# A decoder block: seven pairs of up-projection tiles by Strassen's seven products of quarters

## The chip, the cores and the metric

The kernel runs on one core of a Trainium2 chip. A core has five engines that work side by side, each through its own queue in order: TensorE (PE in the profile; its weight loads are shown as PEld), VectorE (DVE), ScalarE (ACT), GpSimd (POOL) and SyncE (SP, which here only issues DMAs). The metric is the device time of one execution in microseconds (us), lower is better.

## The reference

One decoder block on 512 tokens of width 1024, all in float32. The part that matters here is its last third:

```
h2 = rmsnorm(x, norm2_g) * (1 + scale2) + shift2          # (512, 1024)
u  = causal_dwconv(h2 @ w_up, ffn_conv_w, ffn_conv_b)     # (512, 5632), 3 taps along the tokens
u_gate, u_val = u[..., :2816], u[..., 2816:]
x  = x + gate2 * ((silu(u_gate) * u_val) @ w_down)        # (512, 1024)
return rmsnorm(x, final_g)
```

`shift2`, `scale2` and `gate2` are three of six sections of silu(c) @ w_ada + b_ada. Ahead of this part stand the first norm, a recurrent branch, an attention branch, and their merge; neither the diff nor the prediction touches them.

## The kernel before

**Products of two halves.** Every float32 operand of a large product is split into a high and a low part of TensorE's own float32 format. ScalarE copies the value into the high part, which rounds it; VectorE subtracts that from the value and writes the low part (`split`, lines 200 to 205). A product is then three matmuls: high by high, high by low, low by high (`mm3`, lines 233 to 238). For weights this is done on the fly: SyncE loads 128x1024 of raw weights into one of three buffers (`raw`), and each half of 512 columns is split into a buffer of the names `whl` and `whg`, two of each, in turn (`w_both`, `Stream`).

**The up projection.** Its 5632 output channels are 44 tiles of 128 channels by 512 tokens, taken as 22 pairs j = 0 to 21: tile 2j holds gate channels, tile 2j + 1 the value channels that go with them. A tile is 8 pieces of 128 inputs x 3 matmuls = 24 matmuls of 128 weights by 512 tokens, into one bank of PSUM (the tag `acc`, three banks in turn; `fil`, `gm` and `tr` are other banks). The first four tiles go in two halves of 256 tokens, since the second half of h2 is ready later, so their 192 matmuls are 256 columns wide. From tile 4 on, tiles follow each other in the order of the program (`in_order`).

**Behind each tile** comes the convolution: ScalarE scales the tile out of PSUM and adds the bias (L1050), VectorE adds the two other taps, also out of PSUM (L1052, twice). When both tiles of a pair are through, ScalarE makes tanh of half the gate (L1053), VectorE two multiplications (L1054, L1055), and the product is split into `ff`, the stationary operand of the down projection. That is eleven VectorE instructions for a pair: four splits of weights, four taps, two multiplications, one split of the result.

**The second modulation's row.** gate2 (`ada2(1, ...)`, lines 540 to 555) is summed on VectorE from eight loaded blocks of 128x1024, sixteen instructions (L553), then split, summed over the partitions by four matmuls with ones (L562) and copied out (L563). In this kernel the sums are taken up between pairs 2 and 9, the row behind pair 10.

**What sets the order.** Up to the up projection a table of numbers fixes each engine's order (`QUEUES`). From there on a scheduler orders each engine's queue by priority at build time; loads and splits of weights stand some 100 places ahead (`AHEAD`). On the chip each engine then takes its queue strictly in that order.

Of the kernel before, what the change touches and what calls it, by code (L numbers as in the profile page):

```python
# [87 lines left out]
AHE = 100  # L88
SQB = (1, 0, 2, 3)
EARLY = 4  # L90

QUEUES = {
    "PE": """
# [72 lines left out]
def block_kernel(ctx, tc, a):  # L166
# [860 lines left out]
    with phase("p_ffn") as p3:  # L1027
# [4 lines left out]
        for s in (slice(0, T // 2), slice(T // 2, T)):  # L1032
            for m in range(EARLY):
                for k in range(NK):
                    with tc.high_priority(offset=AHE):
                        w, o = wu.get((m * NK + k) * P)
                    with in_order(ORDE):
                        last = mm3(ub[m][:, s], w, o, P, h2[:, k], s, k == 0, k == NK - 1)
                chained = last
        for j in range(NF):  # L1040
            w = st(sb, "Y", 2, [P, 4, T])
            for i in range(2):
                if 2 * j + i < EARLY:
                    b = ub[2 * j + i]
                else:
                    b = bank("acc")
                    project(b, wu, 2 * j + i, NK, lambda k: h2[:, k], ahead=AHEAD, order=ORD)
                cj = i * NF + j
                u = w[:, i, :]
                S.activation(u, b, AF.Identity, scale=vc("fw", 2 * 2 * NF + cj), bias=vc("fb", cj))  # L1050
                for d in (1, 2):
                    V.scalar_tensor_tensor(u[:, d:], b[:, :T - d], vc("fw", (2 - d) * 2 * NF + cj), u[:, d:], MUL, ADD)  # L1052
            S.activation(w[:, 2, :], w[:, 0, :], AF.Tanh, scale=0.5)  # L1053
            V.scalar_tensor_tensor(w[:, 0, :], w[:, 2, :], 1.0, w[:, 0, :], ADD, MUL)  # L1054
            V.scalar_tensor_tensor(w[:, 0, :], w[:, 0, :], 0.5, w[:, 1, :], MUL, MUL)  # L1055
            o = hl(p3, "ff", NF)
            split(o, 0, T, w[:, 0, :])
            ff.append(o)
# [173 lines left out]
```

## Time and profile before

| | us |
|---|---|
| time, median of 3 runs (lowest to highest) | 877.36 (877.22 to 878.44) |
| the profiled execution: its own time | 880.0 |
| the profiled execution: span of its instructions | 878.2 |
| TensorE busy in the span (share) | 858.8 (98%) |
| VectorE busy | 640.6 (73%) |
| ScalarE busy | 488.1 (56%) |

The profile is one execution. "Busy" is the union of an engine's instructions, and instructions of one engine overlap: a matmul of 512 columns has a duration of 0.40 us, yet the next one starts 0.23 us later. So a duration is a latency, and what an instruction takes of its engine is read from the distance between starts. The share of the span says nothing of one stage; views of stretches do. Lines named L... are those of the kernel before, but in rows of the changed program's order they are three to a hundred higher (`split` is L207 and L208 there).

### The profile page before, as it was taken

Reading aid. Unit: us, or ns where it says so; the run is one execution under the profiler, and the core shown is the slowest. Engines: PE = TensorE matmul, PEld = TensorE weight load, DVE = VectorE, ACT = ScalarE, POOL = GpSimd, SP = SyncE. Lnnn points to the kernel's source line nnn. Section 1 sums busy time; section 2 is a strip of 40 time slices with the busy share of each in tenths; the row PEclk is TensorE's granted clock in tenths of the full one; section 3 lists DMA queues with packets and bytes.
Section 4 is the critical chain, followed back from the end, with each engine's and each line's share of the span. In section 5 each row is a group of like instructions: output and inputs, shape, how many; then the busy total and the mean of one; then the engine's idle time right before and its main releaser. Section 6 shows DMA issues by size and latency. Waiting matters only on the chain.

```text
span 878.2 us, 11212 instructions
## 1 busy us (share of the span) xinstructions
PE 858.8 (98%) x4030; PEld 688.6 (78%) x4030; DVE 640.6 (73%) x1212; ACT 488.1 (56%) x896; POOL 18.7 (2%) x43
## 2 busy tenths in 40 slices
PE   7999999999999999999999999999999999999996
PEld 4777888878876777777877898888788888888885
DVE  7979888987966999997456899666666666424434
ACT  7475778667755788884244654444544444322323
POOL 0001000000020000000000000000000000000000
PEclk8999999999999999999999999999999999999999
DMA  9813233344462343454324174333333332333312
GB/s 351 344 67 106 79 103 119 107 137 120 158 174 96 123 138 123 143 191 146 96 72 144 39 277 125 92 93 95 96 97 97 97 96 82 101 92 94 94 66 97
DMA packets 33804, 109.08 MB, mean 124 GB/s; under 512 B 4290, under 2 KB 8002, under 8 KB 33748
## 3 DMA queue, kind: packets, MB, share of 16 engines
q1 hardware_dynamic: 32116, 103.60, 36.0%
q0 software_dynamic: 1632, 4.75, 2.3%
q8 instruction: 32, 0.52, 0.2%
q14 instruction: 24, 0.20, 0.1%
HBM read 103.59 MB, written 2.13 MB: 120 GB/s over the span
## 4 chain that ended last, share of the span: by engine, by line
PE 72%; DVE 10%; ACT 8%; DMA 7%; issue 3%; POOL 0%; SPq 0%; DVEq 0%; ACTq 0%; POOLq 0%
PE acc L237 9%; PE acc L238 9%; PE acc L236 9%; PE tr L238 3%; PE tr L236 3%; PE tr L237 3%; PE acc L834 2%; PE acc L836 2%; PE acc L835 2%; DMA wa<-in_w_adat 2%; PE tr L738 2%; PE tr L1098 2%; PE tr L1100 2%; PE tr L1099 2%; PE gm L236 2%
## 5 line engine op out<-in xcount | busy, mean ns | idle before, releaser
L205 DVE TENSOR_TENSOR whg<-raw,whg 128x512 fp32r<-128x512 f32 x119 | 81.6, 688 | 86.8 <-ACT whg L204 86.5
L204 ACT ACTIVATE whl<-raw 128x512 fp32r<-128x512 f32 (+2 forms) x131 | 75.2, 576 | 110.8 <-PE acc L238 29.5
L204 ACT ACTIVATE whg<-raw 128x512 fp32r<-128x512 f32 x119 | 74.2, 627 | 98.5 <-PE acc L238 58.6
L205 DVE TENSOR_TENSOR whl<-raw,whl 128x512 fp32r<-128x512 f32 (+2 forms) x131 | 81.3, 621 | 56.2 <-ACT whl L204 55.9
L236 PE MATMUL acc<-A,whg 128*128 128x512 f32 x176 | 70.0, 398 | 0.0
L237 PE MATMUL acc<-A,whg 128*128 128x512 f32 x176 | 69.5, 395 | 0.0
L238 PE MATMUL acc<-A,whg 128*128 128x512 f32 x176 | 69.5, 395 | 0.0
L1052 DVE SCALAR_TENSOR_TENSOR Y<-acc,vec,Y 128x511 f32<-128x511 f32 x86 | 64.4, 749 | 1.3
L238 PE MATMUL acc<-A,whl 128*128 128x512 f32 x160 | 63.2, 395 | 0.0
L237 PE MATMUL acc<-A,whl 128*128 128x512 f32 x160 | 63.2, 395 | 0.0
L236 PE MATMUL acc<-A,whl 128*128 128x512 f32 x160 | 63.1, 395 | 0.0
L715 ACT ACTIVATE P<-P,mx,qsc 128x512 f32<-128x512 f32 (+3 forms) x64 | 41.2, 645 | 17.5 <-DVE mx L711 17.5
L236 PEld LDWEIGHTS acc<-A,whg 128*128 128x128 f32 x176 | 33.0, 187 | 8.4 <-issue 0.2
L238 PEld LDWEIGHTS acc<-A,whg 128*128 128x128 f32 x176 | 33.0, 187 | 8.1
L237 PEld LDWEIGHTS acc<-A,whg 128*128 128x128 f32 x176 | 33.0, 188 | 8.0 <-issue 0.2
L1050 ACT ACTIVATE Y<-acc,vec 128x512 f32<-128x512 f32 x43 | 32.8, 763 | 6.5 <-PE acc L238 6.5
L237 PEld LDWEIGHTS acc<-A,whl 128*128 128x128 f32 x160 | 30.1, 188 | 7.3
L238 PEld LDWEIGHTS acc<-A,whl 128*128 128x128 f32 x160 | 30.0, 188 | 7.1
L236 PEld LDWEIGHTS acc<-A,whl 128*128 128x128 f32 x160 | 30.0, 188 | 7.1
L236 PE MATMUL gm<-A,whg 128*128 128x512 f32 x88 | 35.5, 404 | 0.0
L237 PE MATMUL gm<-A,whg 128*128 128x512 f32 x88 | 35.3, 401 | 0.0
L238 PE MATMUL gm<-A,whg 128*128 128x512 f32 x88 | 35.2, 400 | 0.0
(509 smaller groups left out, 2276.0 us busy)
## 6 DMA issues: line engine op xcount, KB each, us to landing
raw<-in_w_up SPq DMA_DIRECT2D x44, 512.0 KB, 3.5
raw<-in_w_dn SPq DMA_DIRECT2D x22, 512.0 KB, 3.5
wa<-in_w_adat SPq DMA_DIRECT2D x16, 512.0 KB, 9.4
raw<-in_w_adat SPq DMA_DIRECT2D x16, 512.0 KB, 3.3
raw<-in_w_xr SPq DMA_DIRECT2D x10, 512.0 KB, 3.8
raw<-in_w_pr SPq DMA_DIRECT2D x10, 512.0 KB, 3.6
raw<-in_w_gm SPq DMA_DIRECT2D x8, 512.0 KB, 3.6
raw<-in_w_gr SPq DMA_DIRECT2D x8, 512.0 KB, 3.5
```

The costliest lines, as they stand in the source:

```text
L204: S.activation(h, src, AF.Copy)
L205: return V.tensor_tensor(dst[:, 1, lo_c:lo_c + n], src, h.bitcast(F32), SUB).ins
L236: PE.matmul(out, wh, x[:, 0, xs], start=start, stop=False)
L237: PE.matmul(out, wh, x[:, 1, xs], start=False, stop=False)
L238: return PE.matmul(out, wl, x[:, 0, xs], start=False, stop=stop).ins
L715: S.activation(pq, pq, AF.Exp, scale=qsc[:, qb:qb + 1], bias=mx[:, qb:qb + 1], accum_out=sm[:, qb:qb + 1])
L738: PE.matmul(yb[:, kb * P:], vv, pth[:, part, off:off + n], start=(i == 0 and part == 0), stop=(i == 3 and part == 1))
L834: PE.matmul(out, lt[:, 0, s], w[:, 0, :], start=start, stop=False)
L835: PE.matmul(out, lt[:, 0, s], w[:, 1, :], start=False, stop=False)
L836: return PE.matmul(out, lt[:, 1, s], w[:, 0, :], start=False, stop=stop).ins
L1050: S.activation(u, b, AF.Identity, scale=vc("fw", 2 * 2 * NF + cj), bias=vc("fb", cj))
L1052: V.scalar_tensor_tensor(u[:, d:], b[:, :T - d], vc("fw", (2 - d) * 2 * NF + cj), u[:, d:], MUL, ADD)
```

## The change

In pairs j = 5, 7, 9, 11, 13, 15 and 17 the two tiles together, 256 channels by 1024 inputs by 512 tokens, are computed by Strassen's method (Winograd's form of it): weights and h2 are each taken as 2x2 quarters, and seven products of quarters stand in for eight. A product of quarters is 4 pieces x 3 matmuls = 12 matmuls of 256 columns. Four of the seven need sums of quarters of h2 (T1 to T4), computed once during pairs 0 to 3; four need sums of quarters of the weights, computed for each pair. Six products run as one group (`front`); the seventh runs after the gate tile of the next, ordinary pair (`last_product`), because it adds onto a bank that VectorE has to read first. The pair's tiles are put together in SBUF, so the taps of such a pair read SBUF instead of PSUM. The sums for gate2 move from pairs 2 to 9 to pairs 18 to 21, two blocks for each pair, and its row from behind pair 10 to behind pair 21.

```diff
+STRASSEN = (5,7,9,11,13,15,17)
+G2J = 18
+ROOM = -1
...
+        def h_whole(e, n):
+            o = st(p3, "ff", NF, [P, HK, HT])
+            V.tensor_tensor(o, h2[:, HK * e:HK * e + HK, 0, tok2[n]].bitcast(F32),
+                            h2[:, HK * e:HK * e + HK, 1, tok2[n]].bitcast(F32), ADD)
+            return o
...
+        def t_parts():
+            b12, t1 = h_whole(0, 1), h_whole(0, 0)
+            V.tensor_tensor(t1, b12, t1, SUB)
+            yield t_part(t1, p3, "ff", NF)
+            t3 = h_whole(1, 1)
+            V.tensor_tensor(t1, t3, t1, SUB)
+            yield t_part(t1, p3, "ff", NF)
+            V.tensor_tensor(t3, t3, b12, SUB)
+            yield t_part(t3, sb, "R", 4)
+            t4 = h_whole(1, 0)
+            V.tensor_tensor(t4, t4, t1, SUB)
+            yield t_part(t4, sb, "R", 4)
...
+        def prod(out, w, x, start, stop):
+            for k, (xk, s) in enumerate(x):
+                wh, wl = w[:, 0, k * P:k * P + P], w[:, 1, k * P:k * P + P]
+                for e, (we, xe) in enumerate(((wh, 0), (wh, 1), (wl, 0))):
+                    last = PE.matmul(out, we, xk[:, xe, s], start=start and k == 0 and e == 0,
+                                     stop=stop and k == HK - 1 and e == 2, skip_group_check=True).ins
+            return last
+
+        def weights(j):
+            with tc.high_priority(offset=AHEAD):
+                r0, r1 = raw(), raw()
+                dma(r0, a["w_up"][2 * j])
+                dma(r1, a["w_up"][2 * j + 1])
+                w11, w12, w21, w22 = r0[:, :T], r0[:, T:], r1[:, :T], r1[:, T:]
+                s1 = st(p3, "ff", NF, [P, T])
+                q11, q12 = quarter(j, w11), quarter(j, w12)
+                V.tensor_tensor(s1, w21, w22, ADD)
+                V.tensor_tensor(w21, w11, w21, SUB)
+                V.tensor_tensor(w11, s1, w11, SUB)
+                qs1, qs2 = quarter(j, s1), quarter(j, w11)
+                V.tensor_tensor(w12, w12, w11, SUB)
+                qs4, qs3, q22 = quarter(j, w12), quarter(j, w21), quarter(j, w22)
+            return q11, q12, qs1, qs2, qs4, qs3, q22
+
+        def front(w, q11, q12, qs1, qs2, qs4, qs3, q22):
...
+            with in_order():
+                prod(x, q11, h_part(0, 0), True, False)
+                prod(y_, q12, h_part(1, 0), True, True)
+                S.activation(p1, x, AF.Copy)
+                prod(z, qs1, Ts[0], True, False)
+                V.tensor_tensor(w[:, 0, :HT], y_, p1, ADD)
+                prod(x, qs2, Ts[1], False, False)
+                S.activation(p5, z, AF.Copy)
+                prod(z, qs4, h_part(1, 1), False, True)
+                S.activation(p2, x, AF.Copy)
+                V.tensor_tensor(w[:, 0, HT:], z, p2, ADD)
+                chained = prod(x, qs3, Ts[2], False, False)
+                V.tensor_tensor(w[:, 1, HT:], x, p5, ADD)
+            return x, q22
+
+        def last_product(w, x, q22):
+            nonlocal chained
+            with in_order():
+                chained = prod(x, q22, Ts[3], False, True)
+            S.activation(w[:, 1, :HT], x, AF.Copy)
...
         for j in range(NF):
             w = st(sb, "Y", 2, [P, 4, T])
+            if j in STRASSEN:
+                left = (j, w) + front(w, *ahead)
+                continue
+            convs = []
             for i in range(2):
...
+                if left and i == 0:
+                    last_product(*left[1:])
+                    for e in range(2):
+                        conv(left[0], e, left[1][:, 2 + e, :], left[1][:, e, :])
+                    gate(left[1][:, 2, :], left[1][:, 3, :], left[1][:, 0, :])
+                    left = None
+                if i and j + 1 in STRASSEN:
+                    ahead = weights(j + 1)
+                convs.append((j, i, w[:, i, :], b))
+            for c in convs:
+                conv(*c)
+            gate(w[:, 0, :], w[:, 1, :], w[:, 2, :])
+            if j < 4:
+                Ts.append(next(t_it))
-            if j == 2:
+            if j == G2J:
                 g2_it = ada2(1, st(sb, "acc4", 1, [P, D]), lambda: st(sb, "R", 4, [P, D]))
-            if 2 <= j < 10:
+            if G2J <= j < G2J + 4:
+                next(g2_it)
                 g2 = next(g2_it)
-            if j == 10:
+            if j == G2J + 3:
                 ada_row(g2, 1.0)
```

`quarter` splits one quarter of weights into the next `whl` or `whg`; `t_part` splits a T into two tiles; `conv` and `gate` are the instructions of before, put into functions.

The order on TensorE around pair 11 of the changed kernel follows. acc_5857, tr_5858 and tr_5859 are the banks of the Strassen pair, acc_5939 and acc_5997 the gate and value tile of pair 12; ff_4897 to ff_4920 and R_5005 to R_5094 are T1 to T4.

```order
L1099 MATMUL acc_5857<-A_4366,whl_5819 128x256 x12
L1099 MATMUL tr_5858<-A_4366,whg_5822 128x256 x12
L1099 MATMUL tr_5859<-ff_4897,whl_5828 128x256 x6
L1099 MATMUL tr_5859<-ff_4898,whl_5828 128x256 x6
L1099 MATMUL acc_5857<-ff_4919,whg_5831 128x256 x6
L1099 MATMUL acc_5857<-ff_4920,whg_5831 128x256 x6
L1099 MATMUL tr_5859<-A_4366,whl_5835 128x256 x12
L1099 MATMUL acc_5857<-R_5005,whg_5838 128x256 x6
L1099 MATMUL acc_5857<-R_5006,whg_5838 128x256 x6
...
L1099 MATMUL acc_5857<-R_5093,whl_5841 128x256 x6
L1099 MATMUL acc_5857<-R_5094,whl_5841 128x256 x6
L239 MATMUL acc_5997<-A_4366,whl_6000 128x512
```

Where 48 matmuls of 512 columns stood there are 72 of 256, then (where the line of dots is) the gate tile of pair 12, then the last 12 and the value tile.

VectorE's queue of the kernel before around one pair of the same stretch; Y_5984 is the pair that is being finished, Y_5905 the one before it, whl_6067 to whg_6106 are weights of the next.

```order
L1055 SCALAR_TENSOR_TENSOR Y_5905<-Y_5905 128x512
L205 TENSOR_TENSOR whl_6067<-raw_6065,whl_6067 128x512
L205 TENSOR_TENSOR ff_5981<-Y_5905,ff_5981 128x512
L205 TENSOR_TENSOR whg_6070<-raw_6065,whg_6070 128x512
L1052 SCALAR_TENSOR_TENSOR Y_5984<-acc_5985,vec_84,Y_5984 128x511
L1052 SCALAR_TENSOR_TENSOR Y_5984<-acc_5985,vec_84,Y_5984 128x510
L205 TENSOR_TENSOR whl_6103<-raw_6101,whl_6103 128x512
L1054 SCALAR_TENSOR_TENSOR Y_5984<-Y_5984 128x512
L205 TENSOR_TENSOR whg_6106<-raw_6101,whg_6106 128x512
L1052 SCALAR_TENSOR_TENSOR Y_5984<-acc_6021,vec_84,Y_5984 128x511
L1052 SCALAR_TENSOR_TENSOR Y_5984<-acc_6021,vec_84,Y_5984 128x510
```

Splits of weights stand singly between the taps and the multiplications here, with one to three other instructions between one and the next.

The same queue in the changed kernel, from the split of pair 13's second quarter to that of its fourth. Y_5856 is Strassen pair 11, Y_5938 the ordinary pair 12 (its value tile is acc_5997), raw_6030 and raw_6031 are pair 13's raw weights. Its first row is the split of whl_6038, the second quarter; whg_6044 is the third, whl_6047 the fourth.

```order
L208 TENSOR_TENSOR whl_6038<-raw_6030,whl_6038 128x512
L1151 SCALAR_TENSOR_TENSOR Y_5938<-acc_5939,vec_84,Y_5938 128x510
...
L1155 SCALAR_TENSOR_TENSOR Y_5938<-Y_5938 128x512
L1151 SCALAR_TENSOR_TENSOR Y_5856<-Y_5856,vec_84 128x510
L1156 SCALAR_TENSOR_TENSOR Y_5856<-Y_5856 128x512
L1112 TENSOR_TENSOR ff_6034<-raw_6031 128x512
L208 TENSOR_TENSOR ff_5994<-Y_5856,ff_5994 128x512
...
L208 TENSOR_TENSOR whg_6044<-ff_6034,whg_6044 128x512
L1114 TENSOR_TENSOR raw_6030<-ff_6034,raw_6030 128x512
L1151 SCALAR_TENSOR_TENSOR Y_5938<-acc_5997,vec_84,Y_5938 128x511
L1116 TENSOR_TENSOR raw_6030<-raw_6030 128x512
L208 TENSOR_TENSOR whl_6047<-raw_6030,whl_6047 128x512
```

The dots stand for one tap of Y_5856 and for the sum of L1113. Between the second and the fourth quarter of a pair VectorE now finishes two pairs of tiles and forms four sums of weights; before, a split of weights had at most three other instructions ahead of it since the last one.

## Rows read from the trace of the kernel before

**Rows 1.** The page: engine totals, and TensorE, VectorE, clock in 40 slices.

```profile
PE 858.8 (98%) x4030; PEld 688.6 (78%) x4030; DVE 640.6 (73%) x1212; ACT 488.1 (56%) x896; POOL 18.7 (2%) x43
...
PE   7999999999999999999999999999999999999996
...
DVE  7979888987966999997456899666666666424434
...
PEclk8999999999999999999999999999999999999999
```

**Rows 2.** Two stretches: busy us (instructions) of each engine, clock, DMA share, GB/s.

```profile
523.00:545.00 22.00, 22.00 (x97) 17.74 (x96) 22.00 (x36) 11.15 (x18) 0.00 (x0) 1.00 0.44 136
545.00:761.00 216.00, 216.00 (x929) 173.67 (x928) 145.07 (x210) 96.95 (x155) 0.00 (x0) 1.00 0.31 93
```

**Rows 3.** TensorE in order of time: first matmuls of two pairs, 48 apart.

```profile
630.31 0.39 PE L236 MATMUL acc<-A,whl 128*128 128x512 f32 x1
...
641.49 0.39 PE L236 MATMUL acc<-A,whl 128*128 128x512 f32 x1
```

**Rows 4.** TensorE in order of time: 256 columns, 50 matmuls apart.

```profile
500.00 0.28 PE L237 MATMUL acc<-A,ff 128*128 128x256 f32 x1
...
505.88 0.28 PE L236 MATMUL acc<-A,ff 128*128 128x256 f32 x1
```

**Rows 5.** VectorE in order of time where it never waits.

```profile
522.22 0.75 DVE L1052 SCALAR_TENSOR_TENSOR Y<-acc,vec,Y 128x511 f32<-128x511 f32 x1
522.88 0.69 DVE L1055 SCALAR_TENSOR_TENSOR Y<-Y 128x512 f32<-128x512 f32 x1
523.48 0.69 DVE L205 TENSOR_TENSOR whl<-raw,whl 128x512 fp32r<-128x512 f32 x1
...
528.52 0.75 DVE L553 SCALAR_TENSOR_TENSOR acc<-R,cact,acc 128x512 f32<-128x512 f32 x1
529.18 0.69 DVE L1055 SCALAR_TENSOR_TENSOR Y<-Y 128x512 f32<-128x512 f32 x1
```

**Rows 6.** One tile's turn: last matmul of a buffer, ScalarE's split, VectorE's.

```profile
630.07 0.40 PE L238 MATMUL acc<-A,whg 128*128 128x512 f32 x1
...
630.50 0.63 ACT L204 ACTIVATE whg<-raw 128x512 fp32r<-128x512 f32 x1 [1.33 <-PE acc L238]
631.04 0.76 ACT L1050 ACTIVATE Y<-acc,vec 128x512 f32<-128x512 f32 x1
...
631.17 0.69 DVE L205 TENSOR_TENSOR whg<-raw,whg 128x512 fp32r<-128x512 f32 x1 [1.27 <-ACT whg L204]
```

**Rows 7.** VectorE: two taps of one tile, the second waiting for the first.

```profile
631.84 1.53 DVE L1052 SCALAR_TENSOR_TENSOR Y<-acc,vec,Y 128x511 f32<-128x511 f32 x2
```

**Rows 8.** Groups by shape: other widths on VectorE and ScalarE, and the sums for gate2.

```profile
L322 DVE TENSOR_TENSOR crow<-ident,cact 128x1024 f32<-128x1024 f32 x1 | 1.2, 1225 | 0.1
...
L1120 DVE TENSOR_TENSOR Y<-acc,acc 128x256 f32<-128x256 f32 x1 | 0.4, 425 | 0.4 <-PE acc L1100 0.4
...
L204 ACT ACTIVATE pt<-tr 128x256 fp32r<-128x256 f32 x16 | 6.1, 381 | 1.4 <-PE tr L725 1.2
...
L553 DVE SCALAR_TENSOR_TENSOR acc<-R,cact,acc 128x512 f32<-128x512 f32 x16 | 11.6, 746 | 1.5 <-DMA R<-in_w_ada 1.5
```

**Rows 9.** ScalarE at the first convolution, in order of time.

```profile
514.74 0.78 ACT L1050 ACTIVATE Y<-acc,vec 128x512 f32<-128x512 f32 x1 [4.45 <-PE acc L238]
...
519.15 1.28 ACT L1053 ACT_TABLE_LOAD   x1 [0.81 <-DVE Y L1052]
```

**Rows 10.** TensorE in order of time: the first matmul of pairs 2 and 5.

```profile
523.00 0.40 PE L236 MATMUL acc<-A,whl 128*128 128x512 f32 x1
...
556.57 0.39 PE L236 MATMUL acc<-A,whl 128*128 128x512 f32 x1
```

**Rows 11.** The page: DMA issues, KB each, median us to landing.

```profile
raw<-in_w_up SPq DMA_DIRECT2D x44, 512.0 KB, 3.5
```

More of the change, by code (lines that the diff above doesn't have):

```diff
@@ L1039, in block_kernel, with h_part, t_part @@
                 chained = last
+        HT, HK = T // 2, NK // 2
+        tok2 = (slice(0, HT), slice(HT, T))
+        def h_part(e, n):
+            return [(h2[:, HK * e + k], tok2[n]) for k in range(HK)]
+        def h_whole(e, n):
[3 more added lines that the diff above has]
+            return o
+        def t_part(src, pool, tag, bufs):
+            o = [hl(pool, tag, bufs) for _ in range(2)]
+            for i in range(2):
+                split(o[i], 0, T, src.rearrange("p k n -> p (k n)")[:, i * T:i * T + T])
+            return [(o[k // 2], slice(k % 2 * HT, k % 2 * HT + HT)) for k in range(HK)]
@@ new lines, in block_kernel @@
+        Ts = []
+        def t_parts():
[10 more added lines that the diff above has]
+            yield t_part(t4, sb, "R", 4)
@@ new lines, in block_kernel, with quarter @@
+        t_it = t_parts()
+        nq = [0]
+        def quarter(j, src):
+            nq[0] += 1
+            w = hl(p3, "ff", NF) if j <= ROOM else w_both(nq[0])
+            split(w, 0, T, src)
+            return w
+        def prod(out, w, x, start, stop):
[5 more added lines that the diff above has]
+            return last
@@ new lines, in front @@
+        def front(w, q11, q12, qs1, qs2, qs4, qs3, q22):
+            nonlocal chained
+            X, Y_, Z = bank("acc"), bank("tr"), bank("tr")
+            x, y_, z = (b[:, :HT] for b in (X, Y_, Z))
+            p1, p2, p5 = w[:, 2, :HT], w[:, 2, HT:], w[:, 3, :HT]
+            with in_order():
[12 more added lines that the diff above has]
+            return x, q22
@@ new lines, in last_product, with conv @@
+        def last_product(w, x, q22):
+            nonlocal chained
+            with in_order():
+                chained = prod(x, q22, Ts[3], False, True)
+            S.activation(w[:, 1, :HT], x, AF.Copy)
+        def conv(j, i, u, src):
+            cj = i * NF + j
+            S.activation(u, src, AF.Identity, scale=vc("fw", 2 * 2 * NF + cj), bias=vc("fb", cj))
+            for d in (1, 2):
+                V.scalar_tensor_tensor(u[:, d:], src[:, :T - d], vc("fw", (2 - d) * 2 * NF + cj), u[:, d:], MUL, ADD)
@@ L1040, in block_kernel, with gate @@
+        def gate(u0, u1, t):
+            S.activation(t, u0, AF.Tanh, scale=0.5)
+            V.scalar_tensor_tensor(u0, t, 1.0, u0, ADD, MUL)
+            V.scalar_tensor_tensor(u0, u0, 0.5, u1, MUL, MUL)
+            o = hl(p3, "ff", NF)
+            split(o, 0, T, u0)
+            ff.append(o)
+        left = None
         for j in range(NF):
             w = st(sb, "Y", 2, [P, 4, T])
+            if j in STRASSEN:
+                left = (j, w) + front(w, *ahead)
+                continue
+            convs = []
@@ L1047, in block_kernel @@
                     project(b, wu, 2 * j + i, NK, lambda k: h2[:, k], ahead=AHEAD, order=ORD)
[L1048 to L1058, printed above, removed]
-            if j == 2:
+                if left and i == 0:
[3 more added lines that the diff above has]
+                    gate(left[1][:, 2, :], left[1][:, 3, :], left[1][:, 0, :])
+                    left = None
+                if i and j + 1 in STRASSEN:
[7 more added lines that the diff above has]
+            if j == G2J:
                 g2_it = ada2(1, st(sb, "acc4", 1, [P, D]), lambda: st(sb, "R", 4, [P, D]))
-            if 2 <= j < 10:
+            if G2J <= j < G2J + 4:
+                next(g2_it)
                 g2 = next(g2_it)
-            if j == 10:
+            if j == G2J + 3:
                 ada_row(g2, 1.0)
```

## Prediction

> **What bounds the kernel now.** I read the page first: TensorE is busy 98% of the span, VectorE 73%, and the clock stands at its full level in nearly all slices [rows 1]. An average over stages says little, so next I took the busy time by stretches. From 523 to 761 us, where most of the pairs run, TensorE has no idle time at all (22.00 of 22 us, then 216.00 of 216) at a granted clock of 1.00; VectorE is busy 145.07 of 216 us, ScalarE 96.95 [rows 2]. So in this stage only two things move the time: the slots that matmuls take of TensorE, and any new wait of TensorE for the other engines. VectorE has 33% in reserve there, and spends part of it on waits.
>
> **TensorE's slots.** The first matmuls of two pairs, 48 matmuls of 512 columns apart, stand at 630.31 and 641.49: 11.18 us for a pair, 0.233 each [rows 3]. A Strassen pair has 7 products of 4 x 3 matmuls, 84 of 256 columns. Such matmuls are in the trace: fifty of them take 505.88 - 500.00 = 5.88 us, 0.1176 each [rows 4], so 84 take 9.88. That is 1.30 us less for each pair, 9.1 for seven. If 256 columns took exactly half of 512 it would be 84 x 0.1165 = 9.78, and 9.8 for seven.
>
> **What VectorE gets.** Instructions of VectorE overlap: in a stretch without waits they last 0.69 to 0.75 us, but start 0.60 apart, or 0.66 where the operation takes a column of `vec` as its scalar (522.22 to 522.88, then 523.48; the same 0.66 with all operands in SBUF, 528.52 to 529.18) [rows 5]. An ordinary pair has eleven: 4 x 0.66 + 7 x 0.60 = 6.8, some 7.3 with the dependent ones. A Strassen pair and the ordinary pair after it have 13 splits, 4 sums of weights and 4 multiplications (21 x 0.60), 8 taps (x 0.66), and three sums of 256 columns (0.34 each, estimated below): 18.9 us, in 9.88 + 11.18 = 21.06 us of TensorE. Before it was 2 x 7.3 in 22.36. It still fits, at 90%, so what decides is whether single splits come in time.
>
> **The tight place of each pair.** Let a Strassen pair start at 0. Its products take 12 x 0.1176 = 1.41 each; six end at 8.47, the next gate tile at 14.06, the seventh product at 15.47, the value tile and with it the period at 21.07. The order shows that the second quarter of the next Strassen pair goes into the buffer that the seventh product reads. That buffer's turn is in the trace: the last matmul from it starts at 630.07 and ends at 630.47, ScalarE's split starts at 630.50, VectorE's at 631.17, so 0.70 after the end [rows 6]. Thus VectorE's split of the second quarter starts at 15.64 + 0.70 = 16.34. Behind it in VectorE's queue the order of the changed kernel has, itself included, thirteen instructions before the split of the fourth: 9 x 0.60 + 4 x 0.66 = 8.04. Among them are two multiplications and a split that wait for a result of the instruction just before or for ScalarE. Two dependent taps last 1.53 together with 0.75 for the second one, so the first takes 0.78 instead of 0.66 [rows 7]; I add 0.45 for three such places. With 0.73 for the split itself the low part of the fourth quarter is ready at 16.34 + 8.04 + 0.45 + 0.73 = 25.56. It is needed by the third matmul of the fourth product: 21.07 + 3 x 1.41 + 2 x 0.1176 = 25.55. The margin is nil, and a wait in the dependent places can only be larger than I have put it. The fifth quarter comes out at 26.65 for 26.97. I take 0.2 us late for each of the six pairs 7 to 17: **+1.2**, between 0 and 7.2 (1.2 late each, worked out at the third rival).
>
> **The early pairs.** T1 to T4 put eight VectorE instructions of 128x1024 and eight splits into pairs 0 to 3. One such instruction alone lasts 1.225 [rows 8], of which 0.085 overlap the next (0.69 - 0.60), so 1.14; 256 columns last 0.425, so 0.34. That is 9.1 + 4.8 = 13.9 us, where the sums for gate2, 16 x 0.66 = 10.6 us over pairs 2 to 9, leave. The convolutions begin at 514.74, and ScalarE loads its table for tanh at 519.15 for 1.28 us [rows 9]. Two places are close. The bank that tile 7 takes needs the second tap of pair 2's gate tile; pair 2 starts at 523.00 and pair 5 at 556.57 [rows 10], so tile 7 starts at 523.00 + 3 x 5.59 = 539.8, and VectorE's queue up to that tap, at the same prices, ends at 539.9: **+0.15** (0 to 1). And from the first tap (right behind the first bias, 514.74 + 0.78 and 0.03 for the hand-off, 515.55) to the split of pair 5's fifth quarter VectorE has 65 instructions, 8 x 1.14 + 18 x 0.66 + 39 x 0.60 = 44.4 us, plus 3.3 of waits (2.1 for table and tanh, 1.2 for dependent ones and buffers). That ends at 563.25, and with up to 0.2 for the result of the last one I take 563.4. Pair 5 begins 0.15 late, at 556.72 + 0.03, and its fifth product needs the low part 5.65 + 0.24 later, at 562.64: **+0.8** (0 to 3: nothing where the waits are a quarter shorter; 3 where the wide ones cost their whole 1.225, which adds 0.7, and the waits are 5 us).
>
> **The end.** The sums for gate2 now stand in pairs 18 to 21: 7.3 + 4 x 0.66 = 9.9 us of VectorE for each 11.18. The blocks for them, as the raw weights, are asked for far ahead; raw weights land 3.5 us after their issue [rows 11], and a Strassen pair takes the same two. What is left is that the row's matmuls stand in TensorE's queue behind sums that end late: ScalarE's split is ready within 0.1 us of when it is needed. **+0.3** (0 to 1.3).
>
> **Sum.** -9.1 + 0.15 + 0.8 + 1.2 + 0.3 = -6.65. The profiled execution took 880.0 (span 878.2), 0.3% above the median of 877.36; it would become 873.35, and the median 870.7.
>
> **The rivals.**
>
> *Everything is hidden.* The dependent waits are smaller than I put them, and VectorE catches up where it had idle time: -9.1, or 868.3. For it: 10% of VectorE stays free. Against it: a margin of nil at the fourth quarter. Chance 0.17.
>
> *ScalarE's order costs more.* ScalarE copies partial sums out of PSUM between the products. A copy of 256 columns lasts 0.38 [rows 8], but stands in the queue behind splits that take 0.54 (630.50 to 631.04, [rows 6]). VectorE's sum then stands behind the copy and the next splits behind the sum. The splits of the fifth and sixth product are ready only 0.25 and 0.28 early by my walk, so one more split ahead of a copy makes them late. Half a microsecond for each of seven pairs is 3.5: -6.65 + 3.5 = -3.2, or 874.2. Against it: ScalarE is busy less than half of the stage [rows 2]. Chance 0.15.
>
> *VectorE becomes the bound, and the kernel slower.* Place: the same chain of thirteen before the fourth quarter. If these instructions, many of which now follow one on which they depend, cost their whole duration (0.69 and 0.75, [rows 5]) and not the distance, the chain is 13 x 0.09 = 1.2 us longer, so six pairs lose 7.2; pair 5 loses 65 x 0.09 = 5.9. -9.1 + 0.15 + 5.9 + 7.2 + 0.3 = +4.4, or 881.8. It decides from the point where the fourth quarter is late by more than 1 us in each pair. For it: the dependent taps at 0.78 [rows 7]. Against it: neighbours without dependence do start 0.60 apart [rows 5], and the new splits and sums are mostly such. Chance 0.10.
>
> The Trainium skill ("VectorE: DVE Perf Modes", section on the DRAIN) states a rule for this rival: the next operation does not start until the pipe is empty, though one that is not held starts earlier. By its first half every instruction would cost its duration and the time would be this rival's; for neighbours without dependence this trace shows its second half, 0.60 of 0.69.
>
> That the pair still takes the old number of columns is excluded by the order, which has 84 half-width matmuls for 96. The remaining 0.06 goes to mixtures beyond these.
>
> **How the numbers follow.** My forecast has 0.52, and its own range by its bounds is about 868.5 to 873.5. With the first two rivals in it the range is 867.6 (everything hidden and 256 columns at exactly half: -9.8) to 876.0; the slower rival and part of the rest, under 0.2, lie outside. A difference of 0.2%, 1.75 us, is about what measurement can tell from none. Faster by more: the forecast, the first rival, most of the second, 0.80. Slower: most of the third and a little of the rest, 0.10. Between: 0.10.
>
> **What would show it.** In the new trace pairs 7 to 17 should have 84 matmuls 0.118 apart and a period of 21.1 to 21.5 us from one Strassen pair to the next, against 22.36. TensorE's idle time should stand before the third matmul of the fourth product, ended by VectorE's split, and be 0 to 0.5 us for each pair; in pair 5 some 0.8, before the fifth. If idle time is ended by ScalarE, or its place is the fifth or sixth product in all pairs, the second rival is at work. If VectorE is never idle and its starts are 0.69 and more apart, it is the third. The forecast is wrong if the 256-column matmuls take over 0.125 each (0.6 us more a pair) or the median lies above 876.

## The result and the profile after

The changed kernel takes 873.79 us (median of 9 runs) against 878.44 us for the kernel before, run beside it: a ratio of 0.9948 (95% interval 0.9935 to 0.9961), so 4.6 us faster. One of the nine runs, 1176.41 us at a granted clock of 0.655, is left out of the ratio. The forecast was 870.7, with a range of 867.6 to 876.0.

Below is the page of the changed kernel: engine totals, VectorE's busy tenths in 40 slices, and the shares of the chain that ended last.

```profile
PE 852.0 (97%) x4282; PEld 695.0 (79%) x4282; DVE 682.4 (78%) x1298; ACT 513.5 (59%) x953; POOL 18.7 (2%) x43
...
DVE  6988888998965999997465779999999899424434
...
PE 52%; DVE 25%; ACT 9%; DMA 7%; issue 5%; POOL 0%; SPq 0%; ACTq 0%; DVEq 0%; POOLq 0%
```

VectorE's slices 26 to 34 now read 9 and once 8, where 6 stood [rows 1], and a quarter of the chain runs over VectorE (10% before). The stretches of [rows 2], after:

```profile
523.00:545.00 22.00, 21.85 (x99) 17.55 (x98) 21.53 (x31) 12.46 (x21) 0.00 (x0) 1.00 0.29 93
...
545.00:761.00 216.00, 214.44 (x1201) 184.58 (x1200) 192.78 (x310) 121.61 (x211) 0.00 (x0) 1.00 0.35 118
```

The clock is 1.00 as before; VectorE is busy 89% instead of 67%. TensorE's idle time (1.56 us here) understates its waits, since a waiting matmul lets the one ahead of it run out. So I counted the distance between matmuls on both sides of each place and took off the slots between. One ordinary stretch shows how it reads. These are TensorE's rows of pair 11, each product's twelve matmuls in one row:

```profile
623.79 1.58 PE L1099 MATMUL acc<-A,whl 128*128 128x256 f32 x12
625.21 1.56 PE L1099 MATMUL tr<-A,whg 128*128 128x256 f32 x12
626.61 1.58 PE L1099 MATMUL tr<-ff,whl 128*128 128x256 f32 x12
628.02 1.88 PE L1099 MATMUL acc<-ff,whg 128*128 128x256 f32 x12
629.73 1.58 PE L1099 MATMUL tr<-A,whl 128*128 128x256 f32 x12
631.16 1.59 PE L1099 MATMUL acc<-R,whg 128*128 128x256 f32 x12
632.59 0.40 PE L239 MATMUL acc<-A,whl 128*128 128x512 f32 x1
```

Five products take 1.40 to 1.43 us to the next start; the fourth takes 1.71, so it waited about 0.3 us inside. VectorE's queue of the same stretch says for what (the dots leave out taps, multiplications, sums and splits that follow each other with gaps of 0.1 us at most):

```profile
619.20 0.68 DVE L208 TENSOR_TENSOR whg<-raw,whg 128x512 fp32r<-128x512 f32 x1
...
626.45 0.74 DVE L1151 SCALAR_TENSOR_TENSOR Y<-acc,vec,Y 128x511 f32<-128x511 f32 x1
627.11 0.68 DVE L1116 TENSOR_TENSOR raw<-raw 128x512 f32<-128x512 f32 x1
627.71 1.28 DVE L208 TENSOR_TENSOR whg<-raw,whg 128x512 fp32r<-128x512 f32 x2
```

The first of the last two `whg` splits is the fourth quarter's. From the second quarter's split (619.20) to it are 8.51 us; the walk of the prediction had 8.04 + 0.45 = 8.49. The first pair and the second lose more. Pair 5, in its fifth product:

```profile
563.92 0.50 PE L1099 MATMUL tr<-A,whg 128*128 128x256 f32 x2
564.95 1.45 PE L1099 MATMUL tr<-A,whg 128*128 128x256 f32 x10 [0.53 <-DVE whg L208]
```

Two matmuls run, the third waits for VectorE's low part: 1.03 us from 563.92 instead of 0.24. Another 0.3 us was lost in the fourth product. Pair 7, TensorE, and below it ScalarE:

```profile
583.10 1.63 PE L1099 MATMUL tr<-ff,whl 128*128 128x256 f32 x12
585.36 1.81 PE L1099 MATMUL acc<-ff,whg 128*128 128x256 f32 x12 [0.63 <-ACT Y L1129]
```

```profile
583.88 1.15 ACT L207 ACTIVATE whg<-raw 128x512 fp32r<-128x512 f32 x2 [1.58 <-DVE raw L1114]
584.94 0.37 ACT L1129 ACTIVATE Y<-acc 128x256 f32<-128x256 f32 x1
```

The fourth product adds onto the bank of the first, which ScalarE must have copied out (L1129). The copy stands behind two splits of weights, and these wait for a sum on VectorE (L1114).

The table sums the places. Each number is a distance less its slots; for Strassen pairs also less 0.1 us, which the pairs without a wait in the third experiment show.

| us | forecast | measured |
|---|---|---|
| slots of TensorE, seven pairs | -9.1 | -8.5 |
| bank of tile 7 | +0.15 | +0.3 |
| pair 5 | +0.8 | +1.2 |
| pair 7 | +0.2 | +1.1 |
| pairs 9 to 17, 0.13 to 0.30 each | +1.0 | +1.1 |
| the row of gate2 | +0.3 | +0.5 |
| sum | -6.65 | -4.3 |

The sum agrees with the 4.6 us of the runs. The row's 0.5 us hangs on a transfer that came late in this profiled run (experiment 4). The two profiled executions differ by 3.4 only (span 878.2 to 874.8), because the one of after reached pair 2 a microsecond later (523.98 against 523.00 in [rows 10]) through a part that the change does not touch.

### The profile page after: what moved, and what is told of

Read it like the earlier page. It is cut to its first block, busy times and chain, and to the rows that moved or that the text cites. A ratio compares the mean times of both kernels' runs of the same rounds, so it can differ in the third digit from the quotient of the medians.

```text
span 874.8 us, 11864 instructions
## 1 busy us (share of the span) xinstructions
PE 852.0 (97%) x4282; PEld 695.0 (79%) x4282; DVE 682.4 (78%) x1298; ACT 513.5 (59%) x953; POOL 18.7 (2%) x43
## 4 chain that ended last, share of the span: by engine, by line
PE 52%; DVE 25%; ACT 9%; DMA 7%; issue 5%; POOL 0%; SPq 0%; ACTq 0%; DVEq 0%; POOLq 0%
DVE whg L208 4%; DVE whl L208 3%; DVE Y L1151 3%; PE tr L241 3%; PE tr L240 3%; PE tr L239 3%; PE acc L241 2%; PE acc L239 2%; PE acc L240 2%; DMA raw<-in_w_up 2%; PE acc L837 2%; PE acc L839 2%; PE acc L838 2%; PE tr L741 2%; PE tr L1228 2%
## 5 line engine op out<-in xcount | busy, mean ns | idle before, releaser
L208 DVE TENSOR_TENSOR whl<-raw,whl 128x512 fp32r<-128x512 f32 (+2 forms) x138 | 85.6, 624 | 49.7 <-ACT whl L207 49.3
L208 DVE TENSOR_TENSOR whg<-raw,whg 128x512 fp32r<-128x512 f32 x126 | 85.7, 687 | 37.3 <-ACT whg L207 37.0
L239 PE MATMUL acc<-A,whg 128*128 128x512 f32 x120 | 47.9, 399 | 0.0
L240 PE MATMUL acc<-A,whg 128*128 128x512 f32 x120 | 47.4, 395 | 0.0
L241 PE MATMUL acc<-A,whg 128*128 128x512 f32 x120 | 47.4, 395 | 0.0
L1151 DVE SCALAR_TENSOR_TENSOR Y<-acc,vec,Y 128x511 f32<-128x511 f32 (+1 forms) x58 | 42.9, 744 | 3.6 <-ACT Y L1149 3.5
L239 PE MATMUL acc<-A,whl 128*128 128x512 f32 x104 | 41.1, 396 | 0.1
L240 PE MATMUL acc<-A,whl 128*128 128x512 f32 x104 | 41.1, 395 | 0.0
L241 PE MATMUL acc<-A,whl 128*128 128x512 f32 x104 | 41.1, 395 | 0.0
L239 PE MATMUL tr<-A,whl 128*128 128x512 f32 x80 | 32.6, 408 | 1.4 <-ACT whl L207 1.4
L241 PE MATMUL tr<-A,whl 128*128 128x512 f32 x80 | 32.2, 402 | 1.6 <-DVE whl L208 1.4
L711 DVE CUSTOM_DVE_ANT_0 P<-acc,mask 128x384 f32<-128x384 f32 (+3 forms) x64 | 28.6, 485 | 4.5 <-PE acc L708 4.1
L240 PE MATMUL tr<-A,whl 128*128 128x512 f32 x80 | 31.6, 394 | 0.0
L208 DVE TENSOR_TENSOR pt<-tr,pt 128x512 fp32r<-128x512 f32 (+1 forms) x48 | 27.4, 596 | 2.2 <-ACT pt L207 1.6
L741 PE MATMUL tr<-pt,v 128*128 128x512 f32 (+3 forms) x128 | 28.2, 328 | 0.1
L207 ACT ACTIVATE ff<-Y 128x512 fp32r<-128x512 f32 x22 | 13.9, 631 | 23.8 <-DVE Y L1156 23.1
```

The lines of the kernel that those rows point to most:

```text
L207: S.activation(h, src, AF.Copy)
L208: return V.tensor_tensor(dst[:, 1, lo_c:lo_c + n], src, h.bitcast(F32), SUB).ins
L239: PE.matmul(out, wh, x[:, 0, xs], start=start, stop=False)
L240: PE.matmul(out, wh, x[:, 1, xs], start=False, stop=False)
L241: return PE.matmul(out, wl, x[:, 0, xs], start=False, stop=stop).ins
L711: V.tensor_tensor_reduce(out=pt[:, POFF[qd]:POFF[qd] + n], in0=sc[qd], in1=mask[:, T - n:], scale=1.0, scalar=-3e38, op0=ADD, op1=ALU.max, ...
```

## The experiments

Theory 1: TensorE's slots give all they promise, and what comes back is VectorE being late at these places. The rivals: ScalarE's order, VectorE's load as such, or the moved sums. Ratios are to the kernel before, with 95% intervals; "waits" are distances as above, from one profiled run each. "Changed kernel" is the one of the prediction.

**1. The moved sums alone.**

```diff
-STRASSEN = (5,7,9,11,13,15,17)
+STRASSEN = ()
-            if j < 4:
+            if j < 4 and STRASSEN:
```

> Only the sums for gate2 are moved to pairs 18 to 21; no Strassen pair, no T1 to T4. Theory 1 (the saving of 9.1 us in TensorE's slots is made in full, and 4 to 4.5 us of it come back at five places in the second half of the program: the bank of tile 7, 0.3; pair 5, 1.0; pair 7, 1.1; a wait of 0.17 to 0.32 in each of pairs 9 to 17, 1.3; the row of gate2 behind pair 21, 0.6): here only the last place is left, so TensorE waits 0.5 to 0.7 us at the row and nowhere else from pair 2 on, and the time is 0.4 to 0.8 us above the kernel before. Theory 2 (the move itself costs much, since the sums collide with the last pairs): 2 us or more above. Theory 3 (the row is hidden, the wait belongs to the Strassen pairs): no wait at the row, 0 +- 0.4.

Ratio 1.0009 (0.9998 to 1.0019). No wait at the row or anywhere else from pair 2 on. But the edit did not put the sums where its text says. These are the sixteen sums for gate2 in the kernel before, in this run and in the changed kernel (shortest, median and longest in ns, then the first and the last start):

```profile
L553 DVE SCALAR_TENSOR_TENSOR acc<-R,cact,acc x16: 742/745/752, 512.1 to 542.5; 128x512 f32<-128x512 f32 x16
```

```profile
L556 DVE SCALAR_TENSOR_TENSOR acc<-R,cact,acc x16: 742/745/752, 510.9 to 542.0; 128x512 f32<-128x512 f32 x16
```

```profile
L556 DVE SCALAR_TENSOR_TENSOR acc<-R,cact,acc x16: 740/743/751, 703.6 to 736.1; 128x512 f32<-128x512 f32 x16
```

The kernel before has them around pairs 0 to 3, not from pair 2 to 9, and without Strassen pairs they stand there still, whatever pair the program names: the scheduler orders the queue. Only in the changed kernel are they in pairs 18 to 21. So this run moved the row alone, and of the three theories on the sums it decides none.

**2. The same with T1 to T4.**

```diff
-STRASSEN = (5,7,9,11,13,15,17)
+STRASSEN = ()
```

> As the run before, but with the sums T1 to T4 of quarters of h2 and their splits in pairs 0 to 3, which nothing reads: no Strassen pair. Theory 1: the T parts cost TensorE 0.3 us at tile 7's bank, where VectorE's second tap of pair 2's gate tile comes late, and almost nothing else since pair 5 is an ordinary pair again; with the row 0.8 to 1.2 us above the kernel before. Theory 2 (VectorE is so full in pairs 0 to 4 that the T parts alone delay several tiles): more than one wait between pairs 2 and 5 and 2 to 3 us above.

Ratio 1.0005 (0.9996 to 1.0013). The sums for gate2 start at 565.3 to 595.9 us here, so this run too says nothing of their place at the end. One wait, 0.30 us at tile 7's bank (541.06 in the changed kernel, 539.77 here). So that term belongs to the T sums alone, as the walk had it, and they delay nothing else while no Strassen pair follows.

**3. Two VectorE instructions fewer in each pair**, since the second tap of the Strassen pairs' tiles is left out; this kernel does not compute the block.

```diff
-                        conv(left[0], e, left[1][:, 2 + e, :], left[1][:, e, :])
+                        conv(left[0], e, left[1][:, 2 + e, :], left[1][:, e, :], (1,))
```

(`conv` takes the taps as an argument.)

> The changed kernel without the second tap in the fourteen tiles of Strassen pairs: two VectorE instructions fewer in each pair, and one or two fewer between the split of the second and that of the fourth quarter. The convolution of these tiles lacks one tap. Theory 1 (VectorE's queue of thirteen instructions behind a buffer that comes free late sets the wait of the fourth product): the waits of 0.17 to 0.32 us in pairs 9 to 17 disappear, pair 7's falls below 0.6, and the time is 1.5 to 2.3 us below the changed kernel, some 6.3 us below the kernel before. Theory 2 (ScalarE's order of copies and splits sets it): the waits stay within 0.1 us, and the time is within 0.5 us of the changed kernel. Theory 3 (VectorE's total load is the bound): TensorE gains the whole 1.3 us of each pair's two taps, up to 9 us.

Ratio 0.9928 (0.9915 to 0.9940). Tile 7 (0.3) and pair 5 (1.2) are as they were; all waits of pairs 7 to 17 and of the row are gone. TensorE in pair 11:

```profile
623.72 1.58 PE L1099 MATMUL tr<-ff,whl 128*128 128x256 f32 x12
625.14 1.60 PE L1099 MATMUL acc<-ff,whg 128*128 128x256 f32 x12
626.57 1.58 PE L1099 MATMUL tr<-A,whl 128*128 128x256 f32 x12
```

and the splits of the third and fourth quarter on VectorE:

```profile
621.43 0.69 DVE L208 TENSOR_TENSOR whl<-ff,whl 128x512 fp32r<-128x512 f32 x1
...
623.89 0.68 DVE L208 TENSOR_TENSOR whg<-raw,whg 128x512 fp32r<-128x512 f32 x1
```

The fourth product takes 1.43 again. The split starts 2.98 us behind the pair's first matmul (620.91), where it was 3.92; with 0.73 for itself it has to start by 3.75. ScalarE has as many copies and splits as before, so its load was not the cause, in pair 7 neither (its order is the same but for a few instructions that the scheduler moved by some places). The pairs that wait for nothing also give the clean saving. The first matmuls of the gate tiles of pairs 8 and 18:

```profile
587.15 0.40 PE L239 MATMUL acc<-A,whl 128*128 128x512 f32 x1
...
692.89 0.40 PE L239 MATMUL acc<-A,whl 128*128 128x512 f32 x1
```

These are 5 periods of 21.15 us, 1.21 less than 2 x 11.18 [rows 3]; seven are 8.5.

**4. The row of gate2 later.**

```diff
             if j == G2J + 3:
-                ada_row(g2, 1.0)
...
+            if k == 5:
+                ada_row(g2, 1.0)
```

> The changed kernel with the row of gate2 (split, four matmuls with ones, copy) put behind the fifth piece of the down projection instead of ahead of it. Theory 1: the wait of 0.5 to 0.6 us at the first of these matmuls goes, and no other comes, since gate2 is read only behind the first half of the down projection: 0.5 to 0.6 us below the changed kernel. Theory 3 (the wait is only moved to what follows, because VectorE is late there anyway): another wait of 0.4 us or more near the end of the up projection or the start of the down projection, and no change of the time.

Ratio 0.9943 (0.9929 to 0.9956): by time alone no difference from the changed kernel can be told. In the trace the wait at the row is gone and none has come instead. But the edit need not be the reason. In the changed kernel VectorE stood idle ahead of the first sum, until its block of weights had landed; here, with the same order of VectorE's queue up to that sum, it did not. First the changed kernel (issue and sum), then this run:

```profile
697.15 6.26 SPq L552 DMA_DIRECT2D R<-in_w_ada  x3
703.56 0.75 DVE L556 SCALAR_TENSOR_TENSOR acc<-R,cact,acc 128x512 f32<-128x512 f32 x1 [1.48 <-DMA R<-in_w_ada]
```

```profile
694.55 6.26 SPq L552 DMA_DIRECT2D R<-in_w_ada  x3
699.28 0.75 DVE L556 SCALAR_TENSOR_TENSOR acc<-R,cact,acc 128x512 f32<-128x512 f32 x1
```

The first sum starts 6.41 us after the issue there and 4.73 here. From it to the last block's first sum VectorE has 50 instructions in both: 31.18 us without a gap there, 32.42 us here. So it makes up some 1.2 of the delay, and the rest is the wait of 0.5 at the row. Experiments 5 and 9 have the row in its old place and no idle time ahead of the first sum, and wait less than 0.1 us at it. So the 0.5 us come from one late transfer. The traces of experiments 3, 6, 7 and 8 have such idle time ahead of the first sum too (1.5 to 3.2 us), and of these 7 waits at the row, 3 and 6 do not (8 has the row later); what makes the transfer late in some runs stays open.

**5. The T sums on GpSimd**, which is idle there.

```diff
-            V.tensor_tensor(t1, b12, t1, SUB)
+            G.tensor_tensor(t1, b12, t1, SUB)
```

(and so for all eight.)

> The eight sums of 128x1024 for T1 to T4 are computed by GpSimd instead of VectorE. Theory 1 (VectorE's 9 us for them in pairs 0 to 5 make tile 7's bank 0.3 us late and pair 5's fifth quarter 1.2 us late, and the backlog is still there in pair 7): the wait at tile 7 goes, pair 5's falls from 1.2 to below 0.4, pair 7's from 1.1 to that of pair 9 (0.2 to 0.3), and the steady waits of pairs 9 to 17 stay: 1.5 to 2.3 us below the changed kernel, if GpSimd takes under 5 us for each sum (they are needed some 45 us after h2). Theory 2 (pairs 5 and 7 are late because of their own order of copies and splits on ScalarE, not of the T sums): those two waits stay within 0.2 us, gain 0.3 us. Against both: GpSimd's sums slow VectorE's instructions beside them (then VectorE's 0.60 between starts grows there), or come so late that ScalarE's splits of T block its queue: slower than the changed kernel.

Ratio 0.9973 (0.9963 to 0.9984), 2.2 us slower than the changed kernel. The mishap named last came true. GpSimd, then VectorE beside it:

```profile
528.79 2.41 POOL L1076 TENSOR_TENSOR ff<-ff,ff 128x1024 f32<-128x1024 f32 x1 [8.98 <-DVE ff L208]
531.28 2.74 POOL L1078 TENSOR_TENSOR ff<-ff,ff 128x1024 f32<-128x1024 f32 x1
533.99 2.85 POOL L1058 TENSOR_TENSOR ff<-A 128x1024 f32<-128x1024 f32 x1
```

```profile
528.57 0.74 DVE L1151 SCALAR_TENSOR_TENSOR Y<-fil,vec,Y 128x510 f32<-128x510 f32 x1
529.35 2.40 DVE L1156 SCALAR_TENSOR_TENSOR Y<-Y 128x512 f32<-128x512 f32 x1
531.67 2.90 DVE L208 TENSOR_TENSOR whg<-raw,whg 128x512 fp32r<-128x512 f32 x1
534.49 0.74 DVE L1151 SCALAR_TENSOR_TENSOR Y<-acc,vec,Y 128x511 f32<-128x511 f32 x1
535.15 2.23 DVE L208 TENSOR_TENSOR ff<-Y,ff 128x512 fp32r<-128x512 f32 x1
```

VectorE's instructions with two tensors in SBUF last about as long as GpSimd's beside them, 2.2 to 2.9 us instead of 0.69; those that read a tensor from PSUM keep their 0.74. Tile 7 then waits 0.75 and pair 5 3.7 us; pair 7's wait falls to 0.15.

**6. The sums of weights on GpSimd.**

```diff
-                V.tensor_tensor(s1, w21, w22, ADD)
+                G.tensor_tensor(s1, w21, w22, ADD)
```

(and so for all four.)

> The four sums of quarters of weights of each Strassen pair are computed by GpSimd instead of VectorE; T1 to T4 stay on VectorE. Theory 1 (the chain of thirteen VectorE instructions before the fourth quarter sets the steady wait): three of them leave, 1.8 us, so the waits of pairs 9 to 17 go as in the run with one tap left out, 1.1 us in all, and pair 7's 1.1 falls below 0.5; the row's 0.5 goes too, as VectorE has no backlog at pair 18: 1.7 to 2.7 us below the changed kernel, if GpSimd's sum lasts under 1.5 us. Pair 5 stays within 0.5 us of its 1.2. Rival (what matters is when raw weights and buffers arrive, not what VectorE does between): the waits stay. If GpSimd needs 2 us or more for a sum, its four in a row are themselves late at the fourth quarter (raw weights of the value tile land some 4 us before it is needed): 1 us or more of wait in each pair, 5 us slower than the changed kernel.

Ratio 1.0016 (1.0006 to 1.0026). The group of the first of these sums on GpSimd:

```profile
L1112 POOL TENSOR_TENSOR ff<-raw 128x512 f32<-128x512 f32 x7 | 10.2, 1455 | 135.5 <-DMA raw<-in_w_up 135.5
```

1.46 us for what takes VectorE 0.60, and VectorE's splits beside it last up to 1.78. Waits: 0.3 us at tile 7, 1.6 ahead of pair 5, 4.0 in pair 7, 0.7 to 1.3 in each of pairs 9 to 17. The second of these is at the bank of an ordinary tile, for a late tap:

```profile
550.30 0.47 PE L239 MATMUL acc<-A,whl 128*128 128x512 f32 x1 [1.43 <-DVE Y L1151]
```

In pair 11 the one that shows is again ScalarE's copy in its queue (L1135, 0.44 us). Pair 5 waits 0.3 instead of 1.2, but TensorE had waited those 1.6 us just ahead of it, so this does not show that fewer VectorE instructions help it.

**7 and 8. All sums on GpSimd, without and with the row later.** The edits are those above, together.

> Both moves together. Theory 1: the gains add, since they are at different places: no wait of TensorE from pair 2 to pair 21 above 0.1 us beyond what a change between widths costs (0.1 a pair), 4.2 us below the changed kernel, a ratio of about 0.990 to the kernel before; what is left is the saving of slots, 7 x 1.22 = 8.5. Rival: as in the two runs before.

> As the run before, with the row of gate2 also put behind the fifth piece of the down projection. Theory 1: the same as the run before within 0.3 us where VectorE has no backlog at the end, 0.5 us less where it still has.

Ratios 1.0027 (1.0016 to 1.0038) and 1.0032 (1.0021 to 1.0043). No wait at tile 7, 5.9 and 6.0 us in pair 5, about 1 us in each later pair, and in run 7 another 0.7 us at the row. The waits in the traces of runs 6, 7 and 8 add up to 1.4 to 1.8 us more than the times say; what makes up for that stays open.

**9. Six pairs, from 7 on.**

```diff
-STRASSEN = (5,7,9,11,13,15,17)
+STRASSEN = (7,9,11,13,15,17)
```

> Strassen pairs 7 to 17 only, pair 5 by the ordinary way. Theory 1 (pair 5 pays its saving back in a wait of 1.2 us for VectorE's backlog of T sums, and the same backlog makes pair 7's 1.1): pair 7 now comes 22 us behind the last T sum, so its wait is 0.2 to 0.3 as in pair 9; tile 7's 0.3 stays; six savings of 1.22 less 0.3, six waits of 0.2 and the row's 0.5 are 5.3 us below the kernel before, 0.5 to 1.5 us faster than the changed kernel with seven pairs. Rival (pair 7's wait is of the first or second Strassen pair wherever they stand, by ScalarE's order): a wait of 0.8 us or more in pair 7 or 9, and 4 us below the kernel before, the same as seven pairs.

Ratio 0.9924 (0.9910 to 0.9939): one Strassen pair fewer, and 1.4 us faster than the changed kernel by the medians (872.43 against 873.79), 2.1 by the ratios, whose intervals overlap a little; by the waits it is 1.6, of which 0.5 is the row's. Pair 7 is now the first, and has no wait:

```profile
577.73 1.56 PE L1099 MATMUL acc<-A,whg 128*128 128x256 f32 x12
579.13 1.59 PE L1099 MATMUL tr<-A,whl 128*128 128x256 f32 x12
580.56 1.60 PE L1099 MATMUL tr<-ff,whg 128*128 128x256 f32 x12
581.99 1.58 PE L1099 MATMUL acc<-ff,whl 128*128 128x256 f32 x12
583.41 1.58 PE L1099 MATMUL tr<-A,whg 128*128 128x256 f32 x12
```

All starts are 1.40 to 1.43 apart. Pairs 9 to 17 wait 0.15 to 0.26 each. So 1.1 us in pair 7 was the backlog that pair 5 handed on, and pair 5's saving of 1.21 cost 2.3.

**10. Another buffer for the seventh quarter.**

```diff
-                qs4, qs3, q22 = quarter(j, w12), quarter(j, w21), quarter(j, w22)
+                qs4, qs3 = quarter(j, w12), quarter(j, w21); q22 = hl(p3, "ff", NF); split(q22, 0, T, w22)
```

> The changed kernel with the seventh quarter of each pair split into a free buffer of ff instead of the next whl or whg, so that the next pair's second quarter needn't wait until the seventh product has been read. The number of VectorE's instructions is the same. Theory 1 (the wait of the fourth product comes from thirteen instructions behind a buffer that comes free 0.7 us after the seventh product): the chain can start about 1 us earlier, and the waits of 0.2 to 0.3 in pairs 9 to 17 go (1.1 us in all); pair 7's 1.1 falls by 0.5 or more; pair 5, which has no Strassen pair before it, keeps its 1.2. The time is 1 to 2.5 us below the changed kernel. Rival (VectorE's load alone: 90% busy, whatever the buffers): the waits stay within 0.1 us and the time too.

Ratio 0.9947 (0.9932 to 0.9963), nothing gained that can be measured. Pair 7's wait falls to 0.2 and pair 5's to 0.4 (but the seventh product of pair 5 comes 0.9 late); pair 9 has none, pairs 11 to 17 still 0.2 to 0.4. The waits did not go as theory 1 said. VectorE's splits of the second, the seventh and the fourth quarter for pair 13:

```profile
636.17 0.68 DVE L208 TENSOR_TENSOR whg<-raw,whg 128x512 fp32r<-128x512 f32 x1
...
644.19 0.69 DVE L208 TENSOR_TENSOR ff<-raw,ff 128x512 fp32r<-128x512 f32 x1
...
645.40 1.29 DVE L208 TENSOR_TENSOR whl<-raw,whl 128x512 fp32r<-128x512 f32 x2
```

With the buffer free, VectorE's chain does start earlier: 5.21 us ahead of the pair's first matmul (641.38), where it was 4.59 in pair 11 of the changed kernel (619.20 and 623.79). But the scheduler has put the seventh quarter's split ahead of the fourth's, so the chain has fourteen instructions instead of thirteen, and the fourth's split starts 4.02 us behind that matmul, no earlier than the 3.92 of before. The run changes two things that cancel, and what the buffer alone costs stays open.

**11. Pairs 6 to 18.**

```diff
-STRASSEN = (5,7,9,11,13,15,17)
+STRASSEN = (6,8,10,12,14,16,18)
-G2J = 18
+G2J = 19
```

(with the edits of 10 and 4, and the sums for gate2 as 3, 3 and 2 blocks in pairs 19 to 21.)

> Seven Strassen pairs at 6, 8, ... 18 instead of 5, 7, ... 17, the seventh quarter in a buffer of ff, the sums for gate2 in pairs 19 to 21 and their row behind the fifth piece of the down projection. Theory 1: VectorE has one more ordinary pair to catch up behind the T sums, so pair 6's wait is below 0.4 (1.2 in pair 5 before) and the rest have none; only tile 7's 0.3 stays: 7 x 1.22 - 0.3 - 0.4 = 7.8 us below the kernel before, a ratio of 0.991, 3 us faster than the changed kernel. Rival (the sums for gate2 in three pairs, 13.2 us of VectorE in 33 us beside 7.3 a pair, are late): a wait of 1 us or more in pairs 19 to 21 or at the row.

Ratio 0.9923 (0.9908 to 0.9938). Pairs 6 to 12 wait for nothing, 14 to 18 for 0.2 each. But both theories were right: the first bank of the down projection waits for the last tap behind the sums, 1.27 us by distances.

```profile
739.50 0.47 PE L837 MATMUL acc<-whl,ff 128*128 128x512 f32 x1 [1.10 <-DVE Y L1151]
```

**12. As 11, gate2 summed in the down projection.**

```diff
+        ga = st(sb, "A", 1, [P, NK, D])
+        g2_it = ada2(1, st(sb, "acc4", 1, [P, D]), lambda: ga[:, next(ga_it)])
...
+            if k < 8:
+                g2 = next(g2_it)
+            if k == 15:
+                ada_row(g2, 1.0)
```

> As the run with pairs 6 to 18, but the eight blocks for gate2 are loaded into the space of h2 once the up projection has read it, and summed during the first half of the down projection; the row stands behind its fifteenth piece. Theory 1 (the 1.27 us at the first bank of the down projection in the run before were VectorE's backlog of these sums): that wait goes, none takes its place in the down projection, where VectorE was busy 42% at most in the kernel before; the waits left are 0.3 at tile 7 and about 0.6 in the last three Strassen pairs: 8.5 - 0.9 = 7.6 us below the kernel before, 0.9 us below the run before, a ratio of 0.991. Rival (the loads for gate2 stand between those of the down weights in SyncE's queue, which wait until h2 is free): a wait of TensorE of 1 us or more for weights in the first pieces of the down projection, or at the row.

Ratio 0.9917 (0.9898 to 0.9936), 871.44 us: the fastest version by its median, though its interval overlaps those of 9 and 11. No wait at the end of the up projection or in the down projection. Left are tile 7's 0.3 and 0.7 us in pairs 14 to 18. TensorE, VectorE and ScalarE from 545 us to behind pair 18:

```profile
545.00:703.00 158.00, 157.90 (x960) 140.04 (x959) 146.81 (x239) 94.75 (x169) 0.00 (x0) 1.00 0.29 96
```

VectorE is at 93%. I would expect another pair, or anything more of its work here, to be paid for by TensorE; no run tried it.

## Why the prediction was right, and where it was off

- **TensorE full, clock at its level; only slots and new waits count.** Right. The saving is 8.5 us, not 9.1: a pair takes 9.97 us (21.15 - 11.18), not 84 x 0.1176 = 9.88. Its products take 1.40 to 1.44 us where I had 1.41, most of them more; why the spacing of [rows 4] is not quite kept stays open.
- **VectorE's price by distances, 0.60 and 0.66.** Right: the chain of thirteen measured 8.51 for 8.49. So the third rival (whole durations, +4.4) is out. By the rule of the Trainium skill ("VectorE: DVE Perf Modes", The DRAIN you can't avoid) that the next operation waits for an empty pipe, the chain would have been 1.2 us longer; the page's own exception holds here too.
- **The steady place.** Right in place (third matmul of the fourth product, VectorE's low part) and size: 0.13 to 0.30 for 0.2. Of its cause the chain of thirteen is shown (experiment 3: one instruction fewer in it, no wait). That the buffer of the seventh product sets the chain's start is not shown: experiment 10 freed it, but made the chain longer too. The periods from pair 9 on, 21.33 to 21.42 us, lie in the forecast 21.1 to 21.5; the one from pair 7 to pair 9, 22.19, does not.
- **Pair 7.** The step that failed. I walked pair 5 by itself and then a steady period, and gave pair 7 a steady pair's 0.2. It begins with what VectorE has left over from pair 5, and took 1.1. Experiment 9 shows it: without pair 5, no wait.
- **Pair 5 and tile 7.** Places right, 1.2 for 0.8 and 0.3 for 0.15; both within their bounds (3 and 1). Tile 7's cause is shown (experiment 2); that pair 5's is VectorE's backlog of T sums fits experiments 9 and 11, whose first Strassen pair comes one or two pairs later and waits for nothing. The sums for gate2 that make room there stood around pairs 0 to 3, not over pairs 2 to 9 (experiment 1).
- **The end.** 0.5 for 0.3, but not for the reason given, so the size is luck. The split for the row is ready within 0.1 us of its need, as I had it, in experiments 5 and 9. But I took the blocks for gate2 to be asked for far ahead. The first was issued 4.9 us before VectorE was ready for it (697.15 and 702.08) and in this run came 1.48 us too late, which a VectorE without gaps could only in part make up (experiment 4).
- **The second rival** (ScalarE's copies behind splits) appears in the changed kernel in pair 7 and nowhere else, and there as the last link: the splits ahead of the copy wait for VectorE, and the wait goes when VectorE has less to do (experiments 3 and 9).

Together the slots came 0.6 us short and the waits were 1.75 us more than forecast (4.2 for 2.45), of which pair 7 is 0.9: 4.6 us faster for 6.65, and 873.8 for 870.7, inside the range. Of these 3.1 us one is the base: the kernel before took 878.44 beside the changed one, where the forecast started from 877.36. The first rival (everything hidden) is out with the same 4.2 us.

## What to carry to other kernels

Trading one engine's slots for another's work pays until the second engine is full in that stage: here VectorE went from 67% to 89%, and from then on single results came late though the mean still had room. Walk the queue from one period into the next, and begin the walk where the backlog begins (here the T sums), not in a steady period: the first pair cost 2.3 us in waits for 1.2 of saving, and leaving it out was the cheapest improvement. And look in the trace where moved work runs: in experiment 1 the program named other pairs and the sums stayed where they were.

## What the runs showed of the hardware

GpSimd was no free helper. Its 128x512 sum of two tensors in SBUF took 1.46 us where VectorE takes 0.60 from start to start. Its 128x1024 sum took 2.70 where VectorE takes 1.14 (528.25 to 529.38 in the changed kernel). While it ran, VectorE's instructions with two SBUF tensors lasted up to 1.8 us beside the narrow sums and 2.2 to 2.9 us beside the wide ones, instead of 0.69; those with a tensor in PSUM stayed at 0.74. The Trainium skill ("SBUF — State Buffer", Who interferes with whom) has a rule that fits: a VectorE instruction with two SBUF inputs contends with a GpSimd instruction that reads SBUF, over a port pair that is an exclusive lock, and one with at most one SBUF input does not. The trace agrees: in the rows of experiment 5 VectorE's three long instructions end at 531.75, 534.57 and 537.38, each 0.54 to 0.55 us after the GpSimd sum beside them (531.20, 534.02, 536.84), as if each had only then begun its work.
